# Zero rows up to 128 for two attention operands, and two heads by turns in a recurrent solution's scores and products

## The chip, the cores and the metric

The kernel runs on one core of a Trainium2 chip. The metric is the device time of one execution in microseconds (us). Every time in this document is either such a time or is read from the profile of one execution.

## The reference, cut to what matters

Three blocks follow one another on an input of 256 positions by 2048 channels, all in float32. Block 1 is a gated convolution, a gated linear attention and an attention over a memory; block 2 is a sparse attention, a spatial gating and a wide feed-forward; block 3 is a latent attention beside a recurrence in both directions. Three places matter here.

The sparse attention of block 2 picks its keys by an indexer of 8 heads of 64 channels, with one key `ki` for all heads:

```
s = jnp.einsum('bqhd,bsd->bqhs', qib, ki32)
score = jnp.einsum('bqh,bqhs->bqs', wib * idx_scale, jax.nn.relu(s))
```

The latent attention of block 3 has 8 heads. Its scores are a sum of a product over 128 channels and one over 64 rotated (rotary) channels, whose key is again one for all heads:

```
s = (jnp.einsum('bqhd,bkhd->bhqk', qn_b, k_nope) + jnp.einsum('bqhr,bkr->bhqk', qr_b, k_rope))
p = jax.nn.softmax(s * scale, axis=-1)
```

The recurrence of block 3 has 16 heads of 64 channels and runs forwards and backwards over the 256 positions:

```
sa = jnp.einsum('dbhij,dbhj->dbhi', st, a_t)
st = st * w_t[..., None, :] + sa[..., None] * b_t[..., None, :] + v_t[..., None] * k_t[..., None, :]
y = jnp.einsum('dbhij,dbhj->dbhi', st, r_t)
```

## The kernel before, in words

**The stream.** All weights come from one array in the order in which they are used (`run_stream`, line 493). An item is a piece of 512 columns by a 128-row slice. ScalarE rounds it to the type fp32r (`wh`), VectorE makes the rest (`wl`), five items ahead, and TensorE multiplies three times (`wh` and `wl` by the input's `xh`, `wh` by its `xl`) into one of two pairs of banks called `acc`. A finished pair is emptied by a handler.

**The side work.** Everything else is written as generators, called sides, which work in four further banks of PSUM, called `bank`. After each group of three stream matmuls `pump` (line 425) steps through those sides that are ready by the planner's own clock (`Issue`, line 220), which has a cost for each instruction and knows of array tiles only where a call names one (`tile_position`, which halves its cost); it breaks off while that clock has ScalarE or VectorE more than 7.7 us behind TensorE. So the order on each engine is fixed when the program is built. `bank(n)` (line 363) waits until n of the four banks are free, and until the planner's clock is within 0.8 us of the time at which the last of them is read out. A handler that needs a result of the sides calls `need`, which steps sides without any stream matmul until the result is there.

**Attention operands.** `ev_qi` and `ev_ki` (lines 1547 and 1555) make the indexer's operands `qiT` (two heads of 64 channels one above the other in 128 rows) and `kiT` (the one key, twice, one above the other). `indexer` (line 1566) multiplies head by head, each over the 64 rows in which the head lies, two matmuls for a bank. In block 3 `ev_kr`, `ev_wq` and `mla_block` (lines 1959, 1974 and 2026) do the same with `qrT` and `krT`, which lie in the tile `ropes`: for each head a matmul over 128 rows (`kn`, `qn`) and one over 64 rows are added up in one half of a bank.

**The recurrence** is done in two jobs of 8 heads (`job`, line 2191). Within a job the 256 positions are two blocks of 128, and two directions d are worked on together. `scores` (line 2445) makes the matrices `ab` that are to be inverted, four heads for a bank, first the even heads (rows 0 to 63 of the tiles `bk` and `ar`), then the odd ones (rows 64 to 127). `inverses` (line 2517) inverts blocks of 32 on VectorE. `products` (line 2467) makes, for one head and direction a step, three 128 x 128 matrices in one bank (`ps`), which VectorE masks; those of both directions are then multiplied with the values `V` into a bank `wy`, which two heads share; 35 steps. `solve` (line 2581) does the solution by quarters of 32 rows on tiles of 32 x 32 of the array, the two directions by turns. It waits for the inverses, and is begun when the products are done. Last come `early` and `outputs` (lines 2669 and 2689). The second job begins when the solution of the first is done. The stream's weights `br1` need the second job's outputs: `ev_br` (line 2826) and the input `yr1` wait for them.

Of the kernel before, what the change touches and what calls it, by code (L numbers as in the profile page):

```python
# [15 lines left out]
ALU = mybir.AluOpType  # L16
# [623 lines left out]
class Kernel(Builder):  # L640
# [866 lines left out]
    def block2(self):  # L1507
        nc, B = self.nc, self
# [27 lines left out]
        def to_T(e, dst, flag, n=4):  # L1536
# [7 lines left out]
                B.unbank(t)  # L1544
            B.flag(flag)

        def ev_qi(j, acc):
            S["qi_s"] = B.slot([128, 2048], name="qi")
            S["qiT"] = S["qi_s"][:, :1024].rearrange("p (c t) -> p c t", t=256)
            S["kiT"] = S["qi_s"][:, 1024:1280].rearrange("p (c t) -> p c t", t=256)  # L1550
            S["sc"] = S["qi_s"][:, 1280:1792].rearrange("p (b t) -> p b t", t=256)
            B.scaled(S["qiT"], acc, "Rb2")
            B.flag_then("qiT")

        def ev_ki(j, acc):
            e = B.work([128, 256], "nar", 1).rearrange("p (b t) -> p b t", b=2)
            for i in range(2):
                ev_copy(e, acc, 64, 64 * i)
            for b in range(2):
                V.tensor_scalar(out=wi[:, b], in0=acc[b][:, 64:72], scalar1=R[:, b:b + 1], scalar2=512.0 ** -0.5,  # L1560
                                op0=ALU.mult, op1=ALU.mult)
            B.side(to_T(e, S["kiT"], "kiT", 1), True)
            B.side(bias())
            B.side(indexer())

        def indexer():
# [1 line left out]
            yield from B.wait("kiT")  # L1568
            sc = S["sc"]
            for h0 in (0, 4, 1, 5):  # L1570
                p0 = 64 * (h0 % 2)
                for b in range(2):
                    n = 128 * (b + 1)
                    ps, = yield from B.bank()
                    for i in range(2):
                        T.matmul(ps[:, i * n:i * n + n], S["qiT"][p0:p0 + 64, h0 // 2 + i, b * 128:b * 128 + 128],
                                 S["kiT"][p0:p0 + 64, 0, :n], start=True, stop=True)
                    yield
                    t = B.work([128, 512], "sg", 2)
                    A.activation(out=t[:, :2 * n], in_=ps[:, :2 * n], func=AF.Relu)  # L1580
                    B.unbank(ps)
                    for i in range(2):
                        h = h0 + 2 * i
# [309 lines left out]
    def block3(self):  # L1893
# [65 lines left out]
        def ev_kr(j, acc):  # L1959
            d = B.work([128, 256], "nar", 1).rearrange("p (b t) -> p b t", b=2)  # L1960
            ev_copy(d, acc, R, 64)
            S["qrT"] = S["ropes"][:, :1024].rearrange("p (c t) -> p c t", t=256)
            S["krT"] = S["ropes"][:, 1024:1280].rearrange("p (c t) -> p c t", t=256)

            def g():
                yield from B.lock("mix")
# [4 lines left out]
                yield from to_T(d, S["krT"], "krT", 1)  # L1971
            B.side(g(), True)

        def ev_wq(j, acc):
# [51 lines left out]
        def mla_block(b, i0, mp):  # L2026
# [4 lines left out]
            pT = mp[:, 2 * b + 1].rearrange("p (a t) -> p a t", t=128)  # L2031
            for h0 in (i0, i0 + 4):
                hs = (h0, h0 + 2)
                p0 = 64 * (h0 % 2)
# [432 lines left out]
        def products(J):  # L2467


            masks = [B.masks[:, d * 256:d * 256 + 256] for d in range(2)]  # L2470
            seq = [(b, h, d) for b in range(2) for h in range(8) for d in range(2)]
            pend, ready = deque(), deque()
            wy, ms, rb = None, [None, None], [None, None]
            for step in range(35):
                if pend:
                    b, h, d, ps = pend.popleft()
                    m = ms[d] = B.work([128, 2, 128], f"m{d}", 3)
                    if h % 2 == 0:
                        rb[d] = B.work([128, 2, 128], f"rb{d}", 2)
                    V.tensor_tensor(out=m.rearrange("p a t -> p (a t)"), in0=ps[:, :256], in1=masks[d], op=ALU.mult)  # L2480
                    V.tensor_tensor(out=rb[d][:, h % 2], in0=ps[:, 256:384], in1=masks[d][:, :128], op=ALU.mult)
                    B.unbank(ps)
                    if h % 2:
                        B.store(J["rbd"][d][:, 8 * b + h - 1:8 * b + h + 1], rb[d])
                    if d:
                        V.tensor_tensor(out=ms[0][:, 0], in0=ms[0][:, 0], in1=m[:, 0], op=ALU.add)
                        ready.append((step, b, h, ms[0], m))
                out = None
                if ready and ready[0][0] < step:
                    _, b, h, m0, m1 = ready.popleft()  # L2490
                    if h % 2 == 0:
                        wy, = yield from B.bank()
                    vs = J["V"][:, b, h * 64:h * 64 + 64]
                    for i, l in enumerate((m0[:, 0], m0[:, 1], m1[:, 1])):
                        o = i * 128 + h % 2 * 64
                        T.matmul(wy[:, o:o + 64], l, vs, start=True, stop=True)
                    if h % 2:
                        out = wy, b, (h - 1) * 64
                if step < 32:
                    b, h, d = seq[step]  # L2500
                    ps, = yield from B.bank()
                    p, c, ar = at(J, d, b, h)
                    ts = slice(b * 128, b * 128 + 128)
                    T.matmul(ps[:, 256:384], J["bk"][d][p, 0, c, ts], ar[:, 1], start=True, stop=True)
                    T.matmul(ps[:, :256], J["bk"][d][p, 1, c, ts], ar[:, ::-1], start=True, stop=True)
                    pend.append((b, h, d, ps))
                yield
                if out:
                    t, b, o = out
# [476 lines left out]
```

## Time and profile before

| | us |
|---|---|
| median of 3 runs | 3606.69 |
| lowest and highest | 3601.64, 3608.61 |
| the profiled execution, its own time | 3603.35 |
| its span, first to last instruction | 3601.6 |

| engine | busy us | share of the span |
|---|---|---|
| TensorE (PE) | 3561.6 | 99% |
| TensorE weight loads (PEld) | 3063.9 | 85% |
| VectorE (DVE) | 2451.2 | 68% |
| ScalarE (ACT) | 1896.3 | 53% |
| GpSimd (POOL) | 149.0 | 4% |

PEld runs beside PE. A line of a group reads: line, engine, operation, output tile and input tiles by the program's names, rows x columns of the array, rows x elements and type, count; behind the bar busy time in all, then the mean of one in nanoseconds. Most instructions have the same line, 285, since a helper records them, so tiles tell them apart. A float32 matmul leaves two records (two passes), a rounded one leaves one. Records of neighbours overlap, so what one costs is read from start to start.

### The profile page before, as it was taken

To read this page: it belongs to the slowest core of one execution; us is meant where nothing else is said; L and a number is where in the kernel's file an instruction comes from. 1 tells how busy PE (TensorE), PEld (TensorE's weight loads), DVE (VectorE), ACT (ScalarE), POOL (GpSimd) and SP (SyncE) were. 2 spreads that over 40 slices of the span, in tenths; PEclk is the share of its full clock that TensorE was granted. 3 is DMA by queue.
4 is the path that set the end of the run, shared out by engine and by line. 5 is a ranking of instruction groups with operands and counts; after the bars stand their busy time and mean duration, and the time that the engine had idled before them with its cause. 6 is when DMAs were issued, how large, how long until landed. Compare 5 with 4: busy or idle time off the path is not lost.

```text
span 3601.6 us, 56526 instructions
## 1 busy us (share of the span) xinstructions
PE 3561.6 (99%) x20754; PEld 3063.9 (85%) x20754; DVE 2451.2 (68%) x4453; ACT 1896.3 (53%) x3402; POOL 149.0 (4%) x141
## 2 busy tenths in 40 slices
PE   8999999999999999999999999999999999999988
PEld 7889988888988899888879898989888987887767
DVE  7598888886576665555866555555665688587675
ACT  6555556656554545655455544444564653463334
POOL 1000010010000000000200000000000010000000
PEclk9999999999999999999999999999999999999999
DMA  6555556676677765566665555555663655555655
GB/s 236 169 188 157 182 169 197 208 224 187 195 226 222 239 201 179 187 216 217 232 210 182 191 187 190 188 188 187 198 206 115 196 189 182 193 192 170 199 177 186
DMA packets 231774, 698.51 MB, mean 194 GB/s; under 512 B 40708, under 2 KB 51124, under 8 KB 229832
## 3 DMA queue, kind: packets, MB, share of 16 engines
q1 hardware_dynamic: 231496, 694.90, 59.9%
q8 instruction: 162, 2.65, 0.3%
q14 instruction: 116, 0.95, 0.1%
HBM read 661.22 MB, written 36.73 MB: 194 GB/s over the span
## 4 chain that ended last, share of the span: by engine, by line
PE 97%; DVE 1%; DMA 1%; ACT 0%; issue 0%; SPq 0%; DVEq 0%; ACTq 0%
PE acc L285 87%; PE bank L285 10%; DVE wl L285 0%; DMA raw<-in_wstream_dram 0%; DMA x<-f 0%; ACT wh L285 0%; DVE vy L285 0%; DVE o L285 0%; DVE xl L285 0%; DVE rsz L285 0%; ACT junk L285 0%; DVE yst L285 0%; ACT xh L285 0%; DVE x L285 0%; SPq L285 0%
## 5 line engine op out<-in xcount | busy, mean ns | idle before, releaser
L285 DVE TENSOR_TENSOR wl<-raw,wh 128x512 fp32r<-128x512 f32 x2290 | 1569.6, 701 | 1037.1 <-ACT wh L285 1021.4
L285 ACT ACTIVATE wh<-raw 128x512 fp32r<-128x512 f32 x2290 | 1424.3, 629 | 1529.5 <-PE acc L285 975.8
L285 PE MATMUL acc<-wh,xh 128*128 128x512 f32 x3328 | 1327.0, 399 | 7.3 <-ACT xh L285 4.4
L285 PE MATMUL acc<-wh,xl 128*128 128x512 f32 x3328 | 1298.0, 390 | 3.4 <-DVE xl L285 3.4
L285 PE MATMUL acc<-wl,xh 128*128 128x512 f32 x3328 | 1297.1, 390 | 0.0
L285 PEld LDWEIGHTS acc<-wh,xh 128*128 128x128 f32 x3328 | 626.2, 188 | 154.9 <-issue 20.6
L285 PEld LDWEIGHTS acc<-wh,xl 128*128 128x128 f32 x3328 | 626.0, 188 | 135.6 <-DVE xl L285 4.0
L285 PEld LDWEIGHTS acc<-wl,xh 128*128 128x128 f32 x3328 | 626.9, 188 | 121.8 <-DVE wl L285 0.8
L285 PE MATMUL acc<-xh,wh 128*128 128x256 f32 (+3 forms) x2224 | 638.0, 287 | 0.0
L285 PE MATMUL acc<-xh,wl 128*128 128x256 f32 (+3 forms) x2224 | 630.3, 283 | 0.0
L285 PE MATMUL acc<-xl,wh 128*128 128x256 f32 (+3 forms) x2224 | 630.2, 283 | 0.0
L285 PEld LDWEIGHTS acc<-xh,wh 128*128 128x128 f32 (+3 forms) x2224 | 424.3, 191 | 5.5 <-issue 4.0
L285 PEld LDWEIGHTS acc<-xl,wh 128*128 128x128 f32 (+3 forms) x2224 | 424.5, 191 | 1.1
L285 PEld LDWEIGHTS acc<-xh,wl 128*128 128x128 f32 (+3 forms) x2224 | 424.1, 191 | 0.3
L285 DVE SCALAR_TENSOR_TENSOR cacc<-u,cvec,cacc 128x226 f32<-128x226 f32 (+28 forms) x464 | 188.4, 467 | 0.0
L285 PE MATMUL bank<-ar,bk 64*128 64x128 f32 (+1 forms) x384 | 77.4, 328 | 0.0
L285 PEld LDWEIGHTS bank<-ar,bk 64*128 64x128 f32 x384 | 48.6, 187 | 19.2 <-issue 13.4
L285 ACT ACT_TABLE_LOAD x44 | 56.5, 1283 | 3.2 <-DVE mmx L285 1.6
L285 POOL TENSOR_TENSOR msh<-ev 128x508 f32<-128x508 f32 x8 | 10.8, 1346 | 1038.7 <-DVE ev L285 976.3
L285 ACT ACTIVATE junk<-x 128x512 bf16<-128x512 f32 x40 | 25.3, 631 | 36.7 <-DVE x L285 36.3
L285 PE MATMUL acc<-wh,yr 128*128 128x512 f32 x128 | 44.0, 408 | 0.0
L285 POOL TENSOR_TENSOR crstd<-crstd,u 128x256 f32<-128x256 f32 x14 | 21.8, 1560 | 358.6 <-DVE u L285 358.1
(420 smaller groups left out, 2223.8 us busy)
## 6 DMA issues: line engine op xcount, KB each, us to landing
raw<-in_wstream_dram SPq DMA_DIRECT2D x1133, 512.0 KB, 3.9
gate<-sg SPq DMA_DIRECT2D x40, 256.0 KB, 2.2
row<-in_rows_dram SPq DMA_DIRECT2D x38, 256.0 KB, 4.7
sg<-gate SPq DMA_DIRECT2D x24, 256.0 KB, 2.9
sg<-z SPq DMA_DIRECT2D x24, 256.0 KB, 2.6
z<-sg SPq DMA_DIRECT2D x20, 256.0 KB, 2.1
f<-x SPq DMA_DIRECT2D x16, 256.0 KB, 2.5
gt<-gate SPq DMA_DIRECT2D x16, 256.0 KB, 4.1
```

What stands on the lines that cost most here:

```text
L285: r = f(*a, **k)
```

## The change

Indexer keys: `kiT` gets two columns of 256, one for even and one for odd heads; in each the 64 rows of the other heads are zeros, written by GpSimd. The matmuls take all 128 rows of `qiT`. The transposed key is copied in two parts by `halves_T`. `sc` moves in its tile.

Rotary keys: `krT` becomes two tiles of 128 rows in the same way, and the second matmul of each head in `mla_block` takes 128 rows.

Scores: the matmuls of an even and an odd head stand by turns, into two banks that are taken together; both are copied out afterwards.

Products: a step works on two heads of one direction, in two banks that are taken together: first the two matmuls of 128 columns, then the two of 256. 19 steps instead of 35. The work tiles `m` are renamed and counted anew (two buffers for the first direction, one for the second, for each head of the pair). `wy` is filled in one step.

`solve`, `inverses`, `early` and `outputs` are not changed.

```diff
+        def halves_T(e, dst, flag):
+            yield
+            t = yield from B.transposes([e[:, b] for b in range(2)], 128)
+            yield
+            for i in range(2):
+                V.tensor_copy(out=dst[64 * i:64 * i + 64, i], in_=t[64 * i:64 * i + 64, :256])
+            B.unbank(t)
+            B.flag(flag)
...
+            for i in range(2):
+                G.memset(S["kiT"][64 - 64 * i:128 - 64 * i, i], 0.0)
...
-            B.side(to_T(e, S["kiT"], "kiT", 1), True)
+            B.side(halves_T(e, S["kiT"], "kiT"), True)
...
-                        T.matmul(ps[:, i * n:i * n + n], S["qiT"][p0:p0 + 64, h0 // 2 + i, b * 128:b * 128 + 128],
-                                 S["kiT"][p0:p0 + 64, 0, :n], start=True, stop=True)
+                        T.matmul(ps[:, i * n:i * n + n], S["qiT"][:, h0 // 2 + i, b * 128:b * 128 + 128],
+                                 S["kiT"][:, h0 % 2, :n], start=True, stop=True)
...
-            S["krT"] = S["ropes"][:, 1024:1280].rearrange("p (c t) -> p c t", t=256)
+            S["krT"] = [S["ropes"][:, o:o + 256] for o in (1024, 1792)]
+            for i in range(2):
+                G.memset(S["krT"][i][64 - 64 * i:128 - 64 * i], 0.0)
...
-                    T.matmul(o, S["qrT"][p0:p0 + 64, h // 2, tb], S["krT"][p0:p0 + 64, 0], start=False, stop=True)
+                    T.matmul(o, S["qrT"][:, h // 2, tb], S["krT"][h0 % 2], start=False, stop=True)
...
             for b in (0, 1) if d == 0 else (1, 0):
-                for h0 in range(2):
-                    ps, = yield from B.bank()
-                    for i in range(4):
-                        p, c, ar = at(J, d, b, 2 * i + h0)
-                        T.matmul(ps[:, i * 128:i * 128 + 128], bk[p, 0, c, b * 128:b * 128 + 128], ar[:, 0],
-                                 start=True, stop=True)
-                    yield
-                    A.copy(out=av[:, h0::2, b], in_=ps.rearrange("p (i t) -> p i t", t=128))
-                    B.unbank(ps)
+                ps = yield from B.bank(2)
+                for i in range(4):
+                    for h0 in range(2):
+                        p, c, ar = at(J, d, b, 2 * i + h0)
+                        T.matmul(ps[h0][:, i * 128:i * 128 + 128], bk[p, 0, c, b * 128:b * 128 + 128], ar[:, 0],
+                                 start=True, stop=True)
+                yield
+                for h0 in range(2):
+                    A.copy(out=av[:, h0::2, b], in_=ps[h0].rearrange("p (i t) -> p i t", t=128))
+                B.unbank(*ps)
...
-            seq = [(b, h, d) for b in range(2) for h in range(8) for d in range(2)]
+            seq = [(b, c, d) for b in range(2) for c in range(4) for d in range(2)]
...
-            for step in range(35):
+            for step in range(19):
                 if pend:
...
+                    m = [B.work([128, 2, 128], f"m{d}{i}", 2 - d) for i in range(2)]
+                    rb = B.work([128, 2, 128], f"rb{d}", 2)
+                    for i in range(2):
+                        V.tensor_tensor(out=m[i].rearrange("p a t -> p (a t)"), in0=ps[i][:, :256], in1=masks[d], op=ALU.mult)
+                        V.tensor_tensor(out=rb[:, i], in0=ps[i][:, 256:384], in1=masks[d][:, :128], op=ALU.mult)
+                    B.unbank(*ps)
+                    B.store(J["rbd"][d][:, 8 * b + 2 * c:8 * b + 2 * c + 2], rb)
...
+                if step < 16:
+                    b, c, d = seq[step]
+                    ps = yield from B.bank(2)
                     ts = slice(b * 128, b * 128 + 128)
+                    hs = [at(J, d, b, 2 * c + i) for i in range(2)]
+                    for i, (p, _, ar) in enumerate(hs):
+                        T.matmul(ps[i][:, 256:384], J["bk"][d][p, 0, c, ts], ar[:, 1], start=True, stop=True)
+                    for i, (p, _, ar) in enumerate(hs):
+                        T.matmul(ps[i][:, :256], J["bk"][d][p, 1, c, ts], ar[:, ::-1], start=True, stop=True)
+                    pend.append((b, c, d, ps))
```

## Rows read from the trace of the kernel before

**Rows 1.** The page, part 1: busy us, share of the span, instructions.
```profile
PE 3561.6 (99%) x20754; PEld 3063.9 (85%) x20754; DVE 2451.2 (68%) x4453; ACT 1896.3 (53%) x3402; POOL 149.0 (4%) x141
```
**Rows 2.** The page, part 4: the chain that ended last, shares by line.
```profile
PE acc L285 87%; PE bank L285 10%; DVE wl L285 0%; DMA raw<-in_wstream_dram 0%; DMA x<-f 0%; ACT wh L285 0%; DVE vy L285 0%; DVE o L285 0%; DVE xl L285 0%; DVE rsz L285 0%; ACT junk L285 0%; DVE yst L285 0%; ACT xh L285 0%; DVE x L285 0%; SPq L285 0%
```
**Rows 3.** Waits of TensorE: us in total, times, longest.
```profile
PE bank L285 <- DVE vy L285: 16.2, 1, 16.2
```
**Rows 4.** Timeline of TensorE, block 2's attention: start us, length us, record, count.
```profile
1392.60 0.28 PE L285 MATMUL acc<-xh,wl 128*128 128x256 f32 x1
1392.72 1.03 PE L285 MATMUL bank<-kv,qT 128*128 128x256 f32 x4
1393.39 0.47 PE L285 MATMUL acc<-xh,wh 128*128 128x256 f32 x1
1393.70 0.28 PE L285 MATMUL acc<-xl,wh 128*128 128x256 f32 x1
```
**Rows 5.** The same view, an indexer group.
```profile
1302.73 0.28 PE L285 MATMUL acc<-xh,wl 128*128 128x256 f32 x1
1302.94 1.13 PE L285 MATMUL bank<-qi 64*128 64x256 f32 x4
1304.00 0.39 PE L285 MATMUL acc<-xh,wh 128*128 128x256 f32 x1
1304.22 0.28 PE L285 MATMUL acc<-xl,wh 128*128 128x256 f32 x1
```
**Rows 6.** The same view, attention of block 3: one of 16 pairs.
```profile
2742.57 0.70 PE L285 MATMUL bank<-kn,qn 128*128 128x256 f32 x2
2743.20 0.70 PE L285 MATMUL bank<-ropes 64*128 64x256 f32 x2
```
**Rows 7.** The tile qi: durations ns min/median/max, first and last start, forms.
```profile
L285 DVE COPY qi<-bank x1: 418/418/418, 1300.9 to 1300.9; 128x256 f32<-128x256 f32 x1
```
**Rows 8.** Timeline of TensorE around one of 64 products groups.
```profile
2953.63 0.40 PE L285 MATMUL acc<-wl,xh 128*128 128x512 f32 x1
2953.86 0.40 PE L285 MATMUL acc<-wh,xl 128*128 128x512 f32 x1
2954.19 0.92 PE L285 MATMUL bank<-ar,bk 64*128 64x128 f32 x4
...
2955.37 0.39 PE L285 MATMUL acc<-wl,xh 128*128 128x512 f32 x1
```
**Rows 9.** The same view, one of 16 scores groups.
```profile
2935.88 1.16 PE L285 MATMUL bank<-ar,bk 64*128 64x128 f32 x8
...
2937.30 0.39 PE L285 MATMUL acc<-wl,xh 128*128 128x512 f32 x1
```
**Rows 10.** The same view, the solution: six, four and two tiles by turns.
```profile
3071.21 0.73 PE L285 MATMUL bank<-w,ab 32*32 32x64 f32 x48
...
3081.73 0.65 PE L285 MATMUL bank<-w,ab 32*32 32x64 f32 x32
...
3090.70 1.08 PE L285 MATMUL bank<-w,ab 32*32 32x64 f32 x32
```
**Rows 11.** Stretches: length, busy us (count) of PE, PEld, DVE, ACT, POOL; PEclk, DMA.
```profile
2952.00:3063.00 111.00, 111.00 (x518) 82.50 (x517) 89.25 (x188) 39.26 (x71) 3.61 (x4) 1.00 0.60 183
2980.00:3030.00 50.00, 50.00 (x232) 38.54 (x231) 48.19 (x89) 21.17 (x36) 0.00 (x0) 1.00 0.60 194
...
3275.00:3330.00 55.00, 55.00 (x254) 41.67 (x253) 51.47 (x96) 21.59 (x40) 0.00 (x0) 1.00 0.51 161
```
**Rows 12.** Timeline, VectorE then TensorE: end of the inverses, last products of job 0.
```profile
3045.41 0.70 DVE L285 STREAM_TRANSPOSE tl<-tl 128x512 f32<-128x512 f32 x1
...
3063.06 0.78 PE L285 MATMUL bank<-vy,m 128*128 128x64 f32 x6
```
**Rows 13.** Stretch of the wait for vy, columns as in rows 11.
```profile
3458.00:3475.00 17.00, 0.80 (x5) 0.53 (x4) 16.08 (x40) 1.89 (x3) 2.93 (x2) 0.60 0.42 144
```

More of the change, by code (lines that the diff above doesn't have):

```diff
@@ L1549, in ev_qi @@
             S["qiT"] = S["qi_s"][:, :1024].rearrange("p (c t) -> p c t", t=256)
-            S["kiT"] = S["qi_s"][:, 1024:1280].rearrange("p (c t) -> p c t", t=256)
-            S["sc"] = S["qi_s"][:, 1280:1792].rearrange("p (b t) -> p b t", t=256)
+            S["kiT"] = S["qi_s"][:, 1024:1536].rearrange("p (c t) -> p c t", t=256)
+            S["sc"] = S["qi_s"][:, 1536:2048].rearrange("p (b t) -> p b t", t=256)
             B.scaled(S["qiT"], acc, "Rb2")
@@ L1570, in indexer @@
             for h0 in (0, 4, 1, 5):
-                p0 = 64 * (h0 % 2)
                 for b in range(2):
@@ L1970, in g @@
                 B.unlock("mix")
-                yield from to_T(d, S["krT"], "krT", 1)
+                yield
+                t = yield from B.transposes([d[:, b] for b in range(2)], 128)
+                yield
+                for i in range(2):
+                    V.tensor_copy(out=S["krT"][i][64 * i:64 * i + 64], in_=t[64 * i:64 * i + 64, :256])
+                B.unbank(t)
+                B.flag("krT")
             B.side(g(), True)
@@ L2033, in mla_block @@
                 hs = (h0, h0 + 2)
-                p0 = 64 * (h0 % 2)
                 ps, = yield from B.bank()
@@ L2449, in scores @@
             for b in (0, 1) if d == 0 else (1, 0):
-                for h0 in range(2):
-                    ps, = yield from B.bank()
-                    for i in range(4):
-                        p, c, ar = at(J, d, b, 2 * i + h0)
-                        T.matmul(ps[:, i * 128:i * 128 + 128], bk[p, 0, c, b * 128:b * 128 + 128], ar[:, 0],
-                                 start=True, stop=True)
-                    yield
-                    A.copy(out=av[:, h0::2, b], in_=ps.rearrange("p (i t) -> p i t", t=128))
-                    B.unbank(ps)
+                ps = yield from B.bank(2)
[4 more added lines that the diff above has]
+                                 start=True, stop=True)
+                yield
+                for h0 in range(2):
+                    A.copy(out=av[:, h0::2, b], in_=ps[h0].rearrange("p (i t) -> p i t", t=128))
+                B.unbank(*ps)
             J["bk"][d] = bk
@@ L2470, in products @@
             masks = [B.masks[:, d * 256:d * 256 + 256] for d in range(2)]
-            seq = [(b, h, d) for b in range(2) for h in range(8) for d in range(2)]
+            seq = [(b, c, d) for b in range(2) for c in range(4) for d in range(2)]
             pend, ready = deque(), deque()
-            wy, ms, rb = None, [None, None], [None, None]
-            for step in range(35):
+            m0 = None
+            for step in range(19):
                 if pend:
[L2476 to L2484, printed above, removed]
-                    if d:
-                        V.tensor_tensor(out=ms[0][:, 0], in0=ms[0][:, 0], in1=m[:, 0], op=ALU.add)
-                        ready.append((step, b, h, ms[0], m))
@@ new lines, in products @@
+                    b, c, d, ps = pend.popleft()
+                    m = [B.work([128, 2, 128], f"m{d}{i}", 2 - d) for i in range(2)]
+                    rb = B.work([128, 2, 128], f"rb{d}", 2)
+                    for i in range(2):
+                        V.tensor_tensor(out=m[i].rearrange("p a t -> p (a t)"), in0=ps[i][:, :256], in1=masks[d], op=ALU.mult)
+                        V.tensor_tensor(out=rb[:, i], in0=ps[i][:, 256:384], in1=masks[d][:, :128], op=ALU.mult)
+                    B.unbank(*ps)
@@ L2488, in products @@
+                    B.store(J["rbd"][d][:, 8 * b + 2 * c:8 * b + 2 * c + 2], rb)
+                    if d:
+                        for i in range(2):
+                            V.tensor_tensor(out=m0[i][:, 0], in0=m0[i][:, 0], in1=m[i][:, 0], op=ALU.add)
+                        ready.append((step, b, c, m0, m))
+                    else:
+                        m0 = m
                 out = None
                 if ready and ready[0][0] < step:
-                    _, b, h, m0, m1 = ready.popleft()
@@ L2491, in products @@
[L2491 to L2502, printed above, removed]
-                    ts = slice(b * 128, b * 128 + 128)
-                    T.matmul(ps[:, 256:384], J["bk"][d][p, 0, c, ts], ar[:, 1], start=True, stop=True)
-                    T.matmul(ps[:, :256], J["bk"][d][p, 1, c, ts], ar[:, ::-1], start=True, stop=True)
-                    pend.append((b, h, d, ps))
+                    _, b, c, ms, mt = ready.popleft()
@@ new lines, in products @@
+                    wy, = yield from B.bank()
+                    for i in range(2):
+                        vs = J["V"][:, b, c * 128 + i * 64:c * 128 + i * 64 + 64]
+                        for a, l in enumerate((ms[i][:, 0], ms[i][:, 1], mt[i][:, 1])):
+                            o = a * 128 + i * 64
+                            T.matmul(wy[:, o:o + 64], l, vs, start=True, stop=True)
+                    out = wy, b, c * 128
+                if step < 16:
+                    b, c, d = seq[step]
+                    ps = yield from B.bank(2)
+                    ts = slice(b * 128, b * 128 + 128)
+                    hs = [at(J, d, b, 2 * c + i) for i in range(2)]
[4 more added lines that the diff above has]
+                    pend.append((b, c, d, ps))
```

## The prediction

> **What bounds the kernel now.** I read the page's busy shares first: TensorE is busy 99% of the span, VectorE 68%, ScalarE 53%, GpSimd 4% [rows 1]. Then the chain that ended last: nine tenths of it are `acc` matmuls (the streamed weights), a tenth `bank` matmuls, the side work [rows 2]. So a microsecond that leaves TensorE's queue leaves the span, unless another engine is then late. Third, the view of the waits of TensorE: one wait is large, 16.2 us, in which it stands still for VectorE's last work on `vy` [rows 3]; the rest is a few us. Fourth, the timeline around each kind of matmul that the diff touches, and fifth the busy times by stage, to see who is next.
>
> **How a group of matmuls is priced.** TensorE runs in program order, so I take the start of the last `acc` record before a group and of the second one behind it, and subtract two ordinary steps. Each float32 matmul leaves two records, one a pass. With 128 rows, the attention group of two 256-column matmuls takes 1393.70 - 1392.60 - 2 x 0.12 = 0.86 us [rows 4]: 0.43 us for 256 columns, 1.68 ns a column for both passes, and nothing for entering or leaving. The 64-row groups pay more. The indexer's group of the same size has 1.06 us from its first start to the next `acc`, against 0.67 us with 128 rows [rows 5, 4]: 0.39 us for a change of shape in and out (the pause ahead of the one and the slower second step behind the other are 0.09 us each and cancel).
>
> **Part 1, zeros to 128 rows.** In the attention of block 3 each 128-row `kn` matmul is followed by a 64-row `ropes` one, each 2743.20 - 2742.57 = 0.63 us behind the last [rows 6]: a pair takes 1.26 us where two of 128 rows take 0.86. There are 2 x 2 blocks x 2 rounds x 2 heads = 16 pairs: 16 x 0.40 = 6.4 us. The indexer has 8 groups: 8 x 0.39 = 3.1 us (its 128-column half is given the same price, since it is the shape that costs). Added: four GpSimd memsets of at most 64 x 256; POOL is busy 149 us with 141 instructions, 1.1 us each [rows 1], and the memsets are issued a transpose ahead of their first reader, so zero to 1 us; I take 0. Added too: one more VectorE copy for each of the two tiles; the copy takes 418 ns [rows 7] and the indexer's first matmul waits for it: 0.4 us; the rotary one has work ahead of its reader. Net 9.1 us.
>
> **Part 2, two heads by turns.** A products group (64 rows, 128 and 256 columns) costs 2955.37 - 2953.63 - 3 x 0.23 = 1.05 us [rows 8], of which 384 x 1.68 ns = 0.65 are columns. Before there are 2 jobs x 32 = 64 groups, afterwards 32 with twice the matmuls, neighbours in different halves of the array's rows and in different banks. A scores group (four of 128 columns) costs 2937.30 - 2935.88 - 0.23 + 0.10 (the pause ahead, as in rows 8) = 1.29 us [rows 9], 0.86 of it columns; 16 groups become 8. All depends on whether neighbours in different row halves run at the same time. The kernel's solution, which this diff does not touch (it is by quarters of 32 rows already, so that part of the description I price at nothing), shows it [rows 10]: 32 passes of 64 columns last 1.08 us where two tiles take turns, 0.65 us where four do, and 48 passes on six tiles 0.73 us. One after another, 32 passes of half of 64 x 1.68 ns would be 1.72 us in each case. By tile it fits: 16 passes x 0.054 + 0.21 = 1.07, and 8 x 0.054 + 0.21 = 0.64. In the group of six, tiles of different rows share two column blocks and write to two banks, as the heads will. So a doubled group should cost what a single one does: 32 x 1.05 = 33.6 us and 8 x 1.29 = 10.3 us saved. The other end, no overlap: a doubled group is 1.05 + 0.65 = 1.70 and saves 0.40, and 1.29 + 0.86 = 2.15 saves 0.43: 12.8 + 3.4 = 16.2 us. I take the first end, as the six-tile row is the nearest to it; the trace has no two 64-row halves side by side.
>
> Against this speaks the Trainium skill, "TensorE: Matmul & The Clock Gate", Part 3, The mechanism: matmuls start and end strictly in program order, only weight loads are pulled ahead. Then a head's second pass would hold back the other head's first, and only one pass in two would overlap: the products' columns would be about 0.86 instead of 0.65 and the scores' 0.96 instead of 0.86, 7.7 us of saving less. By that rule the 32 passes on four tiles would last about 1.1 us; the row has 0.65 [rows 10], so I go by the row.
>
> Sum for TensorE: 9.1 + 33.6 + 10.3 = 53 us; without overlap 9.1 + 16.2 = 25.3 us.
>
> What moves with it: the products' VectorE work (two masked products a head and direction, one sum a head) keeps its count and size, so do the scores' ScalarE copies and the 32 stores to `rbd` on SP's queue; no DMA is added, and nothing is moved past another queue. The mask that overwrites the now single `m1` buffers waits for matmuls that stand ahead of the ones whose result it reads, so VectorE gets no later wait. What is new is that a step asks for two banks at once of four. A step with a `wy` holds one and has two just given back, so TensorE's pair waits for that step's masks; behind it in TensorE's queue stand the `acc` matmuls.
>
> **What is late next.** (a) VectorE. In the products' stage of the first job it is busy 89.3 of 111 us, and 48.2 of the 50 us in which the inverses run beside it; the second job has 51.5 of 55 [rows 11]. Some ten groups lie in each of these windows, so TensorE would leave them 5 us sooner each and VectorE lets it gain 1.8 and 3.5: 5 us lost. If all product steps crowd in beside the inverses, the whole stage is at VectorE's pace, 89 against 111 - 17 = 94, with bursts: up to 14 us lost. I take 8. (b) The end. The 16.2 us wait is for the last of a chain (products, solution, outputs; job 0, then job 1) that is placed by steps, not by TensorE's time: if it keeps its place in the stream the wait stays, whatever TensorE saves. It moves forward: the inverses of job 0 end at 3045.41 + 0.70, but the last products matmuls stand at 3063.06 [rows 12], and the solution waits for both. The products go from 35 steps to 19. With the inverses as the last, each job's solution starts up to 17 us sooner, 34 us in all for a wait of 16.2 us whose own VectorE work (busy 16.1 of 17 us there [rows 13]) takes longer beside the stream. The clock, granted at 0.60 in those 17 us, would stay up too. Bounds 0 and 18 us; since the shift is larger than the wait but the double steps are longer, I take 12.
>
> Forecast: 53 - 8 + 12 = 57 us. The profiled execution took 3603.35 us, of which 3601.6 are span; 3603.35 - 57 = 3546. The median of the runs shown is 3.3 us above the profiled one: 3550 us.
>
> **The rivals.** *VectorE and the end keep what TensorE gives.* The pairs overlap, but the masks for two heads come at once beside the inverses, 14 us are lost, and the last wait stays: 53 - 14 = 39 us, 3568 us. For it: rows 11. Against: in the other 61 us of that stage VectorE is idle for 20. The Trainium skill states the rule in "TensorEngine Tiling (Array Packing)", PSUM Bottleneck: tiling speeds up TensorE, not the emptying of PSUM, which may then be the bound. The trace agrees so far as VectorE is at 96% in that window. Chance 0.18. *The halves run in line.* Only the changes of shape are saved: 25 us, 3581 us; with the last wait gone, 3565. For it: no row shows two 64-row halves. Against: the six tiles. Chance 0.13. *The chain to the outputs gets longer, and the kernel slower.* Place: a products step that must have two banks while a `wy` holds one, so that each pair waits for VectorE's masks behind the inverses. Price: all that the chain loses is added to the 16.2 us wait. A step now takes 111 / 32 = 3.5 us [rows 11]; to eat 53 us, 26 a job, sixteen double steps must take 137 us, 8.6 us each, two and a half times a single one; from there the kernel is slower, and at 10 us each it would be 3606.7 - 53 + 2 x (160 - 111) = 3652 us. For it: VectorE full for 50 us and only four banks. Against: half as many steps, and a double step adds only one more set of masks. Chance 0.05. *It does not do what it says*: the planner places the steps so that pairs fall apart or the zeros cost a stall at each reader; within 7 us of before. Chance 0.04.
>
> **How the numbers follow.** The forecast has 0.60, with a range of its own from 3535 (53 + 18 saved) to 3562 (the end gives nothing, VectorE takes 8). The range adds the next two cases: 3533 to 3585. Within 0.2% (7 us) is about what a measurement of this kernel cannot tell from no change. Faster by more: 0.60 + 0.18 + 0.13, and a little of the others: 0.92. Same: 0.03. Slower: 0.05.
>
> **What would show it.** Right: 64-row records in 8 groups of 16 (scores) and 32 groups of 8 (products), lasting about what 8 and 4 records last now (1.16 and 0.92 us); in the attention of block 3 no step of 0.63 us; the qi group as short as that of rows 4; the wait for `vy` under 6 us. Wrong: a doubled group of 1.6 us or more (in line); TensorE waiting for `wl` or a bank between 2950 and 3060 by more than 14 us; the wait for `vy` at 16 us or above. The prediction as a whole is wrong if the time is over 3585 us.

## The result, and the profile after

The changed kernel takes 3566.6 us (median of 4 runs, 3563.2 to 3570.8) beside 3605.5 us for the kernel before (median of 4): ratio 0.9893, 95% interval 0.9876 to 0.9910. That is 39 us less, inside the range, but not the 57 us of the forecast: 3568 us was the price of the first rival, in which VectorE and the end keep a part of what TensorE gives. The profiled execution took 3563.33 us, 40.0 less than that of before.

The page after, parts 1 and 4 (the lines that answer to [rows 1, 2]):

```profile
PE 3516.1 (99%) x20754; PEld 3041.9 (85%) x20754; DVE 2450.2 (69%) x4455; ACT 1895.2 (53%) x3402; POOL 149.8 (4%) x145
...
PE acc L285 85%; PE bank L285 7%; DVE wl L285 2%; DVE tmp L285 1%; DVE m L285 0%; SPq L285 0%; ACT wh L285 0%; DMA tl<-td 0%; DMA x<-f 0%; DVE rb L285 0%; DVE vy L285 0%; DMA gh<-z 0%; DVE o L285 0%; DVE sg L285 0%; DVE tl L285 0%
```

TensorE's busy time fell by 45.5 us, more than the span. The share of the side work in the chain fell from 10% to 7%, and VectorE's `wl` (2%) and `tmp` (1%, work of the inverses) have come into it.

TensorE's timeline, a scores group and a products group of two heads (the lines to [rows 9, 8]), a pair of the rotary products and an indexer group [rows 6, 5]:

```profile
2934.18 0.40 PE L285 MATMUL acc<-wh,xl 128*128 128x512 f32 x1
2934.51 1.16 PE L285 MATMUL bank<-ar,bk 64*128 64x128 f32 x16
2935.60 0.50 PE L285 MATMUL acc<-wh,xh 128*128 128x512 f32 x1
...
2955.40 0.39 PE L285 MATMUL acc<-wh,xl 128*128 128x512 f32 x1
2955.72 0.93 PE L285 MATMUL bank<-ar,bk 64*128 64x128 f32 x8
2956.58 0.50 PE L285 MATMUL acc<-wh,xh 128*128 128x512 f32 x1
```
```profile
2739.68 0.59 PE L285 MATMUL bank<-ropes 128*128 128x256 f32 x2
2740.11 0.59 PE L285 MATMUL bank<-kn,qn 128*128 128x256 f32 x2
2740.54 0.59 PE L285 MATMUL bank<-ropes 128*128 128x256 f32 x2
...
1305.33 0.28 PE L285 MATMUL acc<-xh,wl 128*128 128x256 f32 x1
1305.45 1.03 PE L285 MATMUL bank<-qi 128*128 128x256 f32 x4
1306.12 0.47 PE L285 MATMUL acc<-xh,wh 128*128 128x256 f32 x1
```

Twice the matmuls last as long as the single group did: 1.16 us (1.16 before) and 0.93 (0.92). Rotary steps are 0.43 us apart (0.63), the indexer's group takes 0.67 us to the next `acc` (1.06).

Waits of TensorE after (us in total, times, longest; the first line answers to [rows 3]):

```profile
PE bank L285 <- DVE vy L285: 16.2, 1, 16.2
...
PE bank L285 <- DVE rb L285: 1.5, 3, 0.6
PE bank L285 <- DVE qi L285: 0.8, 1, 0.8
PE acc L285 <- DVE wl L285: 0.7, 2, 0.5
```

The wait for `vy` is where it was, to the tenth. Stretches (columns as in [rows 11, 13]) of the products' stages and of that wait:

```profile
2952.00:3036.00 84.00, 81.83 (x456) 63.26 (x456) 73.16 (x159) 34.30 (x63) 1.65 (x1) 1.00 0.65 201
2980.00:3030.00 50.00, 49.42 (x269) 37.87 (x268) 48.61 (x96) 18.56 (x36) 0.00 (x0) 1.00 0.58 190
3228.00:3318.00 90.00, 88.54 (x492) 67.43 (x490) 80.44 (x178) 33.80 (x64) 0.00 (x0) 1.00 0.60 178
```
```profile
3417.00:3434.00 17.00, 0.80 (x5) 0.39 (x4) 16.11 (x41) 1.89 (x3) 2.94 (x2) 0.65 0.45 149
```

TensorE is no longer full while VectorE does the inverses, and it idles through the same 16 us at the end.

**Where the 40 us came from.** Both kernels run the same 17,208 stream matmuls (`acc`) in the same order, so the n-th has a start in either trace, and the difference is the lead gained by then. Places in the order are given by this count below: "after 16461" means that 16461 of them have started.

| stream matmul | place | start before | start after | lead |
|---|---|---|---|---|
| 14000 | behind the indexer | 2700.6 | 2698.4 | 2.2 |
| 15273 | the first job's scores begin | 2935.0 | 2926.5 | 8.4 |
| 15900 | the second job begins | 3163.7 | 3145.3 | 18.4 |
| 16727 | the last ahead of the wait for `vy` | 3457.9 | 3417.1 | 40.8 |
| 17207 | the last | 3589.8 | 3549.8 | 40.0 |

### The profile page after: what moved, and what is told of

Same layout as the page of the kernel before. It is cut to its first block, busy times and chain, and to the rows that moved or that the text cites. A ratio compares the mean times of both kernels' runs of the same rounds, so it can differ in the third digit from the quotient of the medians.

```text
span 3561.6 us, 56530 instructions
## 1 busy us (share of the span) xinstructions
PE 3516.1 (99%) x20754; PEld 3041.9 (85%) x20754; DVE 2450.2 (69%) x4455; ACT 1895.2 (53%) x3402; POOL 149.8 (4%) x145
## 4 chain that ended last, share of the span: by engine, by line
PE 92%; DVE 5%; DMA 1%; issue 1%; ACT 1%; SPq 0%; POOL 0%; DVEq 0%; ACTq 0%; POOLq 0%
PE acc L285 85%; PE bank L285 7%; DVE wl L285 2%; DVE tmp L285 1%; DVE m L285 0%; SPq L285 0%; ACT wh L285 0%; DMA tl<-td 0%; DMA x<-f 0%; DVE rb L285 0%; DVE vy L285 0%; DMA gh<-z 0%; DVE o L285 0%; DVE sg L285 0%; DVE tl L285 0%
## 5 line engine op out<-in xcount | busy, mean ns | idle before, releaser
L285 PE MATMUL bank<-ar,bk 64*128 64x128 f32 (+1 forms) x384 | 41.4, 329 | 1.6 <-DVE rb L285 1.5
L285 PEld LDWEIGHTS bank<-ar,bk 64*128 64x128 f32 x384 | 26.4, 186 | 15.6 <-issue 8.5
L285 ACT COPY w<-bank 32x512 f32<-32x512 f32 (+1 forms) x48 | 24.6, 512 | 15.1 <-PE bank L285 14.6
```

The source lines that it names most:

```text
L285: r = f(*a, **k)
```

## The experiments

Medians beside that of the kernel before in the same set of runs (3605.1 to 3606.1 us); "the changed kernel" is the 3566.6 us above. Runs of one kernel scatter by 2 to 12 us, so differences below some 5 us are read from the traces, place by place. A single trace scatters too: between stream matmuls 15273 and 16727 (start of the one to end of the other: from the first job's scores to the wait for `vy`) run 2 takes 496.2 us and the changed kernel 490.9 with the same instructions.

**1 and 2. Each part alone.** The first keeps the new `kiT` and `krT`, the second the new `scores` and `products`.

> The kernel before with the zero-filled rotary and indexer keys alone (the first six hunks); scores, products and the solution's inputs stay one head a step. Ledger theory (the stream's lead, read at equal places of the stream in the two traces, was 8.4 us when the first job's scores began): 8.2 us less than before, some 3597 us, in the indexer 1.9 and in the rotary products 6.3; TensorE's wait for vy at the end stays at 16.2 us. Rival: the lead was only borrowed from later waits and is given back in the jobs: less than 3 us.

> The kernel before with the two heads by turns in scores and products alone (the last two hunks). Theory 1 (VectorE and the chain behind the inverses keep the end where it is): 32 us less than before, some 3574 us, made up of TensorE's 44 less some 11.5 of waits inside the jobs; the wait for vy stays at 16.2 us. Rival (the parts are not independent: the shorter first part of the kernel is what made VectorE late): over 38 us less, and the wait for vy is under 12 us.

The first took 3597.7 us (ratio 0.9977, 0.9968 to 0.9985): 8.3 less. The second 3575.5 us (0.9915, 0.9901 to 0.9928): 30.5 less. Together 38.8 against 38.9 measured: the parts add up within their scatter, and the wait for `vy` is 16.2 us in both.

**3. One head behind the other.**

```diff
-                for i in range(4):
-                    for h0 in range(2):
+                for h0 in range(2):
+                    for i in range(4):
...
                     for i, (p, _, ar) in enumerate(hs):
                         T.matmul(ps[i][:, 256:384], ...)
-                    for i, (p, _, ar) in enumerate(hs):
                         T.matmul(ps[i][:, :256], ...)
```

> The changed kernel with the same banks and steps, but one head's passes behind the other's in scores and products. Theory (the halves overlap because they are issued by turns; each queue place is taken in order): a products' group goes from 0.55 us between first and last start to between 0.8 and 1.2, a scores' group from 0.89 to between 1.75 and 1.9, in all 15 us more on TensorE if the next head's first passes still start beside the last one's long pass and 28 us more if not; less up to 10 that the waits for VectorE hide: 3572 to 3594 us. Rival (passes of one half are held apart by tile, so that the order within a group doesn't matter): spans as in the changed kernel, time within 2 us of it.

3571.0 us (0.9901, 0.9886 to 0.9916), 4.4 more than the changed kernel, with intervals that overlap. Its timeline, a scores and a products group:

```profile
2939.99 1.71 PE L285 MATMUL bank<-ar,bk 64*128 64x128 f32 x16
...
2942.52 0.93 PE L285 MATMUL bank<-ar,bk 64*128 64x128 f32 x8
```

The products group is as short as by turns, the scores group 0.55 us longer: 8 x 0.55 = 4.4 us, as much as the medians differ. Between first and last start a products group has 557 ns (550 by turns), a scores group 1437 (890). Single records show why: in the scores group the second head's first pass starts at 554 ns, beside the fifth of the first head's eight, and in the products group at 14 ns, beside the first of four. So TensorE starts a pass ahead of its turn, past the three passes before it, when its half of the rows is free. The rival was right for the products, where my theory had 0.8 to 1.2 us; for the scores neither was, since 1.44 us lies between the rival's 0.89 and the theory's 1.75 to 1.9. The Trainium skill, "TensorE: Matmul & The Clock Gate", Part 3, The mechanism, has matmuls start and end strictly in program order; here they don't, and by that rule the group in line would have lost its overlap almost wholly.

**4. No arithmetic in the inverses.** The lines from `for t in range(1, 16)` to the last `tensor_reduce` go.

> The changed kernel without the arithmetic of the inverses (the multiplications and sums between the load of tl and the store of td2, 50 instructions and some 29 us of VectorE a job); the solution then multiplies with the identity. Theory 1 (the inverses, VectorE's work, set where the second job's solution stands in the stream, and with it the end): the second solution begins some 170 stream matmuls (37 us) earlier, the wait for vy goes from 16.2 us to under 1, the waits inside the jobs shrink too: 3540 to 3551 us. Rival 2 (a slot or a load in the stream holds the solution, or the chain from the solution to vy is itself the long part): the wait for vy stays above 10 us and the time above 3556 us.

3542.1 us (0.9821, 0.9807 to 0.9834), 24.5 less than the changed kernel. The wait for `vy` is gone and the second solution begins after stream matmul 16287 instead of 16461. Between stream matmuls 15273 and 16727 it takes 489.3 us against 490.9, and from the start of 16727 to that of the last 112.6 us against 132.7: nearly all of the gain is the end. Theory 1 holds, rival 2 falls: what lies behind the inverses is not too long in itself.

**5. The inverses first.** `B.side(inverses(J))` becomes `B.side(inverses(J), True)`.

> The changed kernel with the inverses ahead of the products in the list of side work. Theory 1 (both need VectorE and the solution needs both, so whichever goes first pushes the other back): the inverses end some 20 places of the stream earlier and the products' end later, the second solution begins within 6 places of where it was, the wait for vy is 16 us, the time within 2 us of the changed kernel's 3566.6. Rival (the inverses, now last, hold the solution alone): the solution comes forward by their lag of some 20 places and the time falls by 4 us.

3569.6 us (0.9893, 0.9877 to 0.9910): no difference clear of the scatter. The inverses of the second job end at stream matmul 16416 instead of 16436, but its last products matmuls stay at 16437, although its scores begin 18 places earlier; the solution still begins at 16461, and the wait is 16.2 us. In the first job the inverses stay where they were, the products end 30 places later, and so the solution begins 30 later. So the inverses do not hold the solution alone: what they gain the products lose.

**6. The sum of the directions in PSUM.**

```diff
-                        for i in range(2):
-                            V.tensor_tensor(out=m0[i][:, 0], in0=m0[i][:, 0], in1=m[i][:, 0], op=ALU.add)
...
-                        for a, l in enumerate((ms[i][:, 0], ms[i][:, 1], mt[i][:, 1])):
+                        for a, l, st, sp in ((0, ms[i][:, 0], True, False), (0, mt[i][:, 0], False, True),
+                                             (1, ms[i][:, 1], True, True), (2, mt[i][:, 1], True, True)):
```

**7. The same instructions, placed earlier.** In `Issue.take` VectorE's cost is multiplied by 0.9 from the first job on; **8** is both.

```diff
-            cost = 0.07 + n * (0.0065 if name == "reciprocal" else 0.00105)
+            cost = (0.07 + n * (0.0065 if name == "reciprocal" else 0.00105)) * self.dve
```

> The changed kernel with the sum of the two directions' masked products made in PSUM: VectorE's 16 additions of 128x128 a job (0.28 us each, 4.5 us a job) go, TensorE has 16 more 64-column passes a job. Theory 3 (a step's chain of VectorE instructions, one behind the other in the written order, sets when the solution is put into the stream): the second solution begins some 95 stream matmuls (20 us) earlier, the wait for vy falls from 16.2 us to some 5 to 9, TensorE pays some 4 us for its extra passes: 3557 to 3562 us. Theory 1 in its hard form (VectorE's throughput alone): 9 us of VectorE come free over two jobs, so the end moves by at most 9 less 4: 3561 to 3567 us. Rival 2 (the chain behind the solution sets the end): the wait stays at 16 us, 3570 us.

> The changed kernel with the same instructions, but in the list by which the order is written VectorE's instructions cost a tenth less from the first job on, so that the second solution is put 117 stream matmuls (25 us) earlier. Theory 1 in its hard form (VectorE is full between the first products and the solution): the wait for vy goes, but TensorE waits as long inside the jobs: within 4 us of the changed kernel's 3566.6. Theory 3 (the order was written too far apart, VectorE had time left): the wait for vy goes to under 2 us and less than 5 us come up elsewhere: 3550 to 3556 us.

> The sum in PSUM and the order written with VectorE's instructions a tenth cheaper, together; the second solution begins some 168 stream matmuls (36 us) earlier than in the changed kernel. Theory 3: no wait for vy, and by 4 us of extra passes slower than the order alone, 3553 to 3560 us. Theory 1 in its hard form: with 9 us of VectorE's work gone it waits less inside the jobs than the order alone, and comes out up to 5 us faster than it.

The sum in PSUM: 3557.2 us (0.9862, 0.9847 to 0.9877). The order alone: 3560.3 us (0.9870, 0.9855 to 0.9885). Both: 3566.6 us (0.9891, 0.9877 to 0.9906). Waits of TensorE, of the sum in PSUM, then of the order alone:

```profile
PE bank L285 <- DVE vy L285: 2.7, 1, 2.7
```
```profile
PE bank L286 <- DVE rb L286: 8.1, 8, 1.5
```

With the sum in PSUM the second solution begins 96 stream matmuls (some 20 us) earlier, for 9 us less of VectorE's work in two jobs, and the wait shrinks by 13.5 us. A group of passes into `wy` lasts 1.90 us instead of 1.45 (16 of them: 7.2 us), but the stretch from 15273 to 16727 only from 490.9 to 492.7 us, since TensorE idles 2.0 us in it instead of 4.4. With the order alone the wait is gone, but that stretch takes 507.0 us: 12.9 us idle, eight waits for `rb` among it. The part behind it gets 18.9 us shorter, so the two traces differ by only 2.9 us where the medians differ by 6.3. So neither theory 3 nor the hard form of theory 1 is the whole: an earlier place in the order is worth what VectorE can keep up with. Both together are slower than either alone, which neither theory had foreseen: the stretch takes 514.5 us, 7.5 more than with the order alone, about the 7.2 us of the extra passes, and TensorE idles 12.3 us in it instead of 12.9. VectorE's 9 us less bought next to nothing there.

**9 and 10. GpSimd takes a share of VectorE's work.**

```diff
-                nc.vector.tensor_tensor(
+                e = nc.gpsimd if self.part and ns % 3 == 0 else nc.vector
+                e.tensor_tensor(
                     out=wl[:, :size], in0=src, in1=wh[:, :size].bitcast(F32), op=ALU.subtract
```

> The changed kernel with every third of the stream's wl subtractions on GpSimd from the first job's scores to the second job's inverses; VectorE loses some 0.7 us for each, TensorE gets no pass more. The second solution begins 99 stream matmuls earlier than in the changed kernel, 3 from where it begins with the sum in PSUM. Theory 3 (VectorE's work, as the order counts it, places the solution; the end follows the place): the wait for vy falls to some 3 us as there, and without the extra passes (some 4 to 7 us) the time is 3549 to 3555 us. Rival (GpSimd's 1.3 to 1.6 us for 128x512, and its use of the same memory beside VectorE, make wl late and VectorE slower): TensorE waits for wl by 10 us or more, VectorE's masked products take over 0.45 us, 3560 us or more.

> As the run with every third, but every second subtraction on GpSimd, and the two heads' sums in one VectorE instruction. The second solution begins 147 stream matmuls (32 us) earlier than in the changed kernel. Theory 3 with time left on VectorE: no wait for vy, 3546 to 3552 us. Rival (the order is now ahead of what VectorE does, as in the run with VectorE counted a tenth cheaper): the wait for vy is gone but 5 to 10 us of waits for rb, w and tl come up inside the jobs, 3553 to 3560 us. Rival (GpSimd late): waits for wl of 10 us or more, over 3560 us.

Every third: 3570.3 us (0.9907, 0.9892 to 0.9922), a miss, although the second solution stands where the sum in PSUM had put it. Every second with the merged sum: 3560.2 us (0.9875, 0.9858 to 0.9891); the wait for `vy` is gone, and waits for `rb` (3.7 us), `wl` (3.2) and others come up in the jobs, much as its first rival had it. The two timelines of the run with every third, VectorE and then GpSimd:

```profile
2965.49 0.48 DVE L285 TENSOR_TENSOR m<-m,m 128x128 f32<-128x128 f32 x2
2965.89 1.29 DVE L285 TENSOR_TENSOR tmp<-tl 128x32 f32<-128x32 f32 x1
2967.22 0.19 DVE L285 TENSOR_REDUCE tl<-tmp 128x8 f32<-128x32 f32 x1
2967.44 1.01 DVE L285 TENSOR_TENSOR tmp<-tl 128x50 f32<-128x50 f32 x1
```
```profile
2965.69 1.42 POOL L285 TENSOR_TENSOR sg<-sg 128x512 f32<-128x512 f32 x1 [8.67 <-DMA sg<-vsh]
2967.07 1.27 POOL L285 TENSOR_TENSOR wl<-raw,wh 128x512 fp32r<-128x512 f32 x1
```

A multiplication of 32 elements that takes 0.21 us elsewhere takes 1.29 and ends 0.07 us behind the first of GpSimd's two; the next but one takes 1.01 and ends 0.11 us behind the second. From 2930 to 3330 us, 33 of VectorE's instructions are longer than their shortest like by over 0.3 us, 29.4 us in all; in the changed kernel there is one. All but two of the 33 read two operands in SBUF, 17 of them are the subtractions that VectorE kept. The 60 subtractions that went would have been 60 x 0.69 = 41 us. The masked products, which read a bank, stay at 0.41 us, and TensorE's waits for `wl` are 3.1 us: of the rival's two signs one was right in kind (VectorE slower), but in other instructions than it named. The Trainium skill, "SBUF — State Buffer", SBUF: two separate sides, calls the port that these two engines share an exclusive lock, taken by a VectorE instruction with two SBUF inputs against a GpSimd one; the trace agrees in both points, but for the two instructions with one operand.

**11 and 12. The blocks to be inverted lie transposed.** Every engine's order stays that of the changed kernel (11) or of run 7 (12).

```diff
-                V.transpose(out=flip[qs], in_=ab[1][qs, :, qs])
+                V.transpose(out=flip[qs], in_=ab[0][qs, :, qs])
...
-                V.tensor_tensor(out=tv, in0=pair(tt, 0, (32, t), (1, t)), in1=pair(tin, t, (0, t), (32, t)), op=ALU.mult)
+                V.tensor_tensor(out=tv, in0=pair(tt, 0, (32, t), (1, t)), in1=pair(tin, 32 * t, (0, t), (1, t)), op=ALU.mult)
```

> The changed kernel with every engine's instructions in the same order, but the blocks to be inverted lie transposed in tl (the other direction is flipped), so that 19 of the inverses' multiplications a job read neighbours where they read every 32nd element. These take 2.0 ns an element in the changed kernel, 12.2 us a job, where VectorE's sums take 1.04: about 5.3 us of VectorE a job should go. Theory 3 (the place of the second solution in the written order sets the end): the wait for vy stays at 16 us, the waits inside the jobs lose 1 to 4 us, 3562 to 3566 us. Theory 1 in its hard form (VectorE's throughput sets the end): up to 10.6 us less, 3556 to 3560 us. Rival (the repeated operand or the short runs make these instructions slow, not the stride): their durations and the time stay, 3566 us.

> The same transposed blocks in the order written with VectorE's instructions a tenth cheaper from the first job on (there the wait for vy was gone and TensorE waited for VectorE inside the jobs). Theory 3 (place and throughput together): the 10.6 us that VectorE gets back shorten the waits inside the jobs by 5 to 10 us: 3550 to 3556 us. Rival (those waits come from the order itself, a step's results asked for too soon behind their matmuls): within 3 us of 3560.

The first job's 19 multiplications (durations in ns: shortest, median, longest; first and last start), in the changed kernel and in run 11:

```profile
L285 DVE TENSOR_TENSOR tmp<-tl x19: 163/545/2072, 2960.7 to 3004.5; 128x2 f32<-128x2 f32 x1, 128x8 f32<-128x8 f32 x1, 128x18 f32<-128x18 f32 x1, 128x32 f32<-128x32 f32 x1
```
```profile
L285 DVE TENSOR_TENSOR tmp<-tl x19: 162/366/1226, 2958.8 to 2998.9; 128x2 f32<-128x2 f32 x1, 128x8 f32<-128x8 f32 x1, 128x18 f32<-128x18 f32 x1, 128x32 f32<-128x32 f32 x1
```
```profile
PE bank L285 <- DVE vy L285: 16.2, 1, 16.2
```

They take 8.2 us a job instead of 12.2, and the last instruction of the first job's inverses starts 104.2 us behind stream matmul 15273 instead of 108.0, yet the solution begins at the same stream matmul and the wait for `vy` is the same 16.2 us (last line, run 11): the place in the written order decides, not the time at which VectorE is done. The median is 3559.5 us (0.9871, 0.9857 to 0.9886), in the range that theory 1 in its hard form had. The traces don't bear that out: the wait is unchanged, the profiled run is only 3.8 us below that of the changed kernel, 1.5 of it between 15273 and 16727 and 2.5 between 7000 and 14000, where the two kernels have the same instructions. The two intervals overlap, so a gain of run 11 is not shown. Run 12 takes 3553.5 us (0.9858, 0.9842 to 0.9875), 52 below the kernel before and the fastest version with the whole computation: the stretch takes 497.8 us instead of 507.0, more than the 5 us by which it scatters, and TensorE idles 8.9 us in it instead of 12.9, as theory 3 had it.

| kernel | second solution after stream matmul | wait for `vy` | 15273 to 16727 | idle in it | median |
|---|---|---|---|---|---|
| before | 16455 | 16.2 | 523.3 | 0.0 | 3605.5 |
| changed | 16461 | 16.2 | 490.9 | 4.4 | 3566.6 |
| 5 inverses first | 16461 | 16.2 | 493.8 | 5.9 | 3569.6 |
| 11 transposed | 16461 | 16.2 | 489.5 | 4.2 | 3559.5 |
| 6 sum in PSUM | 16365 | 2.7 | 492.7 | 2.0 | 3557.2 |
| 9 every third on GpSimd | 16362 | 7.2 in two | 505.6 | 12.9 | 3570.3 |
| 10 every second on GpSimd, merged sum | 16314 | none | 507.9 | 12.7 | 3560.2 |
| 7 order | 16344 | none | 507.0 | 12.9 | 3560.3 |
| 12 transposed, order | 16344 | none | 497.8 | 8.9 | 3553.5 |
| 8 sum in PSUM, order | 16293 | none | 514.5 | 12.3 | 3566.6 |
| 4 no inverses | 16287 | none | 489.3 | 2.6 | 3542.1 |

In every run with the wait of 16.2 us, that of the kernel before too, the second solution ends after the same stream matmul, 16683; with the sum in PSUM it ends after 16593, with the order alone after 16542.

## Why the prediction was right or wrong

**The overlap: right.** Two halves of 64 rows run at the same time without a loss; "in line" was wrong, and run 3 shows that not even the order by turns was needed for the products. "TensorE runs in program order" does not hold for passes of different halves within a group (run 3). The 7.7 us that the prediction gave to matmuls in program order are 0.21 x 32 + 0.10 x 8 = 7.5 by its own numbers.

**Part 1: right, some 0.9 us too high.** Forecast 9.1, measured 8.3 alone and 8.4 in the lead. Kernels with the same instructions up to there reach the first job up to 6.5 us apart, so the terms are read where they arise: stream matmuls 6000 to 7000 (the indexer) take 151.4 us before and 149.5 after, 14000 to 15273 (the rotary products) 234.4 and 228.1, and run 1 has 149.6 and 228.1. That is 1.9 us for 2.7 and 6.3 for 6.4. In the indexer TensorE waits 0.8 us for the copies of `qi` where I took 0.4.

**Part 2 on TensorE: the size was off.** I priced a products group at 1.05 us and 32 of them at 33.6. Over all groups (start of the next `acc`, less that of the last one, less a step of 0.217 us; medians) a single one cost 0.95 and a double one 0.96, scores 1.19 and 1.20. The 0.1 was the slower step behind the group, and it was not won: the stream's own steps between 15273 and 16727 take 346.3 us before and 346.0 after, with 26 groups fewer among them. And I had left out that two heads' passes into `wy`, now in one group, cost 1.27 us where two groups cost 0.62 each. So 64 x 0.95 - 32 x 0.96 = 30.1, 16 x 1.19 - 8 x 1.20 = 9.4, and 32 x 0.62 - 16 x 1.27 = -0.5 for `wy`: 39.0 instead of 43.9.

**VectorE late: right.** Forecast 8 (5 to 14). The stretch gained 32.4 us of these 39.0: 6.6 lost, 4.4 of it seen as idle time of TensorE. Run 2 against run 1, the same pair of kernels in that stretch, gained 28.7 (496.2 for 524.9): some 10 lost, so the term is known to a few us, inside the bounds.

**The end moves forward: this step failed.** I had written "With the inverses as the last, each job's solution starts up to 17 us sooner", and took 12 us for a wait that then stayed at 16.2, which was one of my signs of being wrong. The inverses did become the last in the first job, but because they moved back (TensorE, then VectorE; the lines to [rows 12]):

```profile
3029.05 1.45 PE L285 MATMUL bank<-vy,m 128*128 128x64 f32 x12
...
3034.50 0.71 DVE L285 STREAM_TRANSPOSE tl<-tl 128x512 f32<-128x512 f32 x1 [3.89 <-DMA tl<-td]
```

Their last instruction comes after stream matmul 15585 instead of 15554, in the second job after 16436 instead of 16392. I had left them at their old place while pulling the products' work of two heads a step into the same stretch of VectorE. The first solution begins 30 stream matmuls earlier; 12 are left at its end, 6 when the second job begins, and the second solution begins 6 later and ends where it did. Overlooked as well: the arithmetic of the inverses ends 10 to 14 us before that last instruction (at 3031.5 us before, 3022.2 after), since their result is stored and loaded back in between (VectorE sits idle for 3.89 us until that load, as the line shows); in run 11 it is still 13.1 us. Runs 5, 6 and 11 show what holds it: its place in an order that was fixed with the planner's costs for VectorE. Less work as the planner counts it (6) or a lower price (7) moves the end; work that merely runs faster on the chip (11), or comes in another succession (5), does not.

In sum 8.4 + 39.0 - 6.6 = 40.8 us, less 0.8 lost behind the wait, where 9.1 + 43.9 - 8 + 12 = 57 were forecast: 12 of the 17 missing are the end. The first rival's time came true, half of its mechanism with it: the end kept its wait, but VectorE took 7 to 10 and not 14. That the time lies in the stated range is luck as far as the forecast goes: the forecast's own range ended at 3562 us, and only the rivals' part of it reaches 3567.

What stays open: why the price of an order written too early is as high as runs 7 and 8 show (the stretch is 16 and 24 us longer than in the changed kernel, TensorE's idle time in it only 8 more, and 7 us of run 8 are the extra passes), and whether run 11 gains anything. No run changed the planner's price for TensorE, a rival that is left: it adds a cost for each matmul of a doubled group, as if the halves ran one after the other, so it does not see what the overlap saves.

## What to carry to other kernels

When an order is written at build time, a wait at its end is moved by the place of the work in that order: ask what the planner's costs make of a change before counting on the time at which an engine will be free. After a speed-up of one engine, take work off the next one first and only then place things earlier: the order alone gave 3 (traces) to 6 us (medians), with 8 us less of VectorE's work 10 to 13. Work that is only handed on to another engine did not do it here: with passes handed to TensorE (8) the two together gave nothing, and a third of the subtractions on GpSimd (9) made the jobs longer. Price a group from the median of all its like and count what a merge puts into one group, not only what it takes out.

## What the runs showed of the hardware

- In run 3 TensorE started a pass ahead of its turn when the half of the rows that it needs was free, past three passes of the other half: 554 ns into a group of sixteen whose first eight passes need the other half, 14 ns into one of eight.
- In run 9 a VectorE instruction with two operands in SBUF waited for a running GpSimd instruction to its end and took up to 1.13 us longer; the masked products, which read a bank, took at most 0.43 us beside it.
- A VectorE multiplication of float32 took 2.07 us for 1024 elements with one operand read at every 32nd element (changed kernel), 1.23 us with neighbours (run 11).
